# Two lows of the output projection by accumulating transfer, sums ahead of a low in the paired gates, and a pause in the early up weights

## The chip, the cores and the metric

The kernel runs on one core of a Trainium2 chip. The metric is the device time of one execution in microseconds (us), median of three runs. The engines of the core work side by side, each through an instruction queue of its own: TensorE (PE, with its weight loads as PEld), VectorE (DVE), ScalarE (ACT), GpSimd (POOL) and SyncE (SP). SP issues most transfers. POOL issues those that add to their destination.

## The reference

One layer of a hybrid backbone runs on 128 context tokens and 512 latent tokens, 640 in all, at width 1024, in f32. Cut to what matters:

```python
merged = (g_a * (y_a @ lw['w_br_a']) + g_b * (y_b @ lw['w_br_b'])
          + g_c * (y_c @ lw['w_br_c']) + g_d * (y_d @ lw['w_br_d']))
return merged @ lw['w_o'], kh, vh, s_f, s_b
...
mix, kh, vh, s_f, s_b = token_mixers(h, lw, lb_f, lb_b, ctx_k, ctx_v, s0_f, s0_b)
x = x + g1 * mix
h = rmsnorm(x, lw['norm2_g']) * (1.0 + sc2) + sh2
x = x + g2 * conv_ffn(h, lw['w_up'], lw['ffn_conv_w'], lw['ffn_conv_b'], lw['w_down'])
```

The gates `g_a` to `g_d` are sigmoids of `h @ w_gate`. The products touched by the change are the gates with their branch products, and `merged @ w_o`. After them come the second norm and the product with `w_up`.

## The kernel before

Every f32 product is made of three matmuls. An operand x is split in a high part, a copy of x in the matmul's type (ACT), and a low part, x minus the high part (DVE, `low`). High by high, high by low and low by high are summed in PSUM.

Weights come from HBM through a staging tile `raw` (three buffers, pool `rp`) into a tile `w` (three buffers, pool `wp`) that holds high and low. A raw buffer is free for the next load when both parts have been made. For some weights of the input projection the low part is made another way: `low_dma` lets ACT write minus x into the low half rounded to the matmul's type like the high half, and a transfer issued by POOL adds x to it, which leaves the remainder.

*The work list.* `units` holds a load, a preparation and a computation for each weight tile. `ahead` starts loads up to four units ahead and preparations up to two units ahead. Unless an instruction is pinned in program order, the framework's planner sets the order of each engine's queue from its own estimates; TensorE's queue also follows that planned order.

*The pair stage* (`g_all`, `g_pair`). Fourteen pairs of gate tiles are computed, each by seven block products for the gate (`gprod`, 12 matmuls) and seven small ones for the branch (`bprod`, 3 matmuls). This needs, besides the weight blocks A (the first staging tile as it is loaded) and C, sums of blocks: s0 and s1 (operand S, copied by `g_b` into B), and two further sums written over b12 and b21. While pair p runs, the operands of pair n = p + 1 are made: `g_a`, `g_sums`, `g_b`, `g_c`, `g_zh`, `g_zl`. In this stage ACT's, DVE's and POOL's instructions made through `oact`, `ovec` and `opool` are pinned in the order of the code. A pair that opens a new branch (`new`) also splits that branch's values (`y_split`), and makes g_b later.

*The output projection* (`wo_tile`). `w_o` is cut in two halves of 512 columns (nh) and four blocks of 256 rows (kk_). In the first half each block is used as it comes: its six matmuls for each of five row blocks t of 128 tokens, in five PSUM accumulators, one in a bank of the pool m, and four in two tiles of the pool g, of which row blocks 1 and 3 share one, 2 and 4 the other. With the last block the sums are read out by DVE: `wt`, the product with the gain `g1`, and the addition to x2. In the second half nothing is computed until its fourth block has come, and then each row block takes all four. Block (1,0) lies in region MG0; (1,1), (1,2) and (1,3) take the three wp buffers that (0,1), (0,2) and (0,3) leave. `R["half"]` is set when the first half's last matmul has been put in the program.

*Beside it* runs `up_early`, a generator stepped as the program is written. It prepares the first weights of the up projection ahead of time: it loads them, splits them, makes their block sums, and stores the split operands to DRAM (`upd`) in six parts, for lack of room, in regions XL0 and XL1, which are used twice. For pair 1 it waits until `half`. After each finished row block of the second half `norm2` is started: square, root, scaling into C, transposes on TensorE, modulation and split. Then `up_all` loads the next up weights by the same raw buffers.

Of the kernel before, what the change touches and what calls it, by code (L numbers as in the profile page):

```python
# [13 lines left out]
ALU = mybir.AluOpType  # L14
# [56 lines left out]
def tile_step(ctx: ExitStack, tc: tile.TileContext, a: dict, outs: list, dbg=None):  # L71
# [58 lines left out]
    def region(tag, shape, dt=F32):  # L130
        return big.tile(shape, dt, tag=tag, name=nm(tag))
# [25 lines left out]
    ovec, opool, oact = Ordered(nc.vector), Ordered(nc.gpsimd), Ordered(nc.scalar).activation  # L157
# [938 lines left out]
    def y_split():  # L1096
        bi = gx["bi"]
        c, y = gx["C"], R["y" + BR[bi]]
        src = [gx["Y"][:, i * HC:j * HC] for i, j in ((0, 2), (3, 4), (2, 3))]
        dst = [[c[:, h, 0:2].rearrange("p i t -> p (i t)"), c[:, h, 2], y[:, h, 0, HC:T]] for h in range(2)]  # L1100
        for o, x in zip(dst[0][:2], src):
            oact(o, x, AF.Copy)
        lows = [(l, x, h) for h, l, x in zip(dst[0], dst[1], src)]
        return lows[:2], lows[2]
# [26 lines left out]
    def low(w, x, h):  # L1131
        ovec.tensor_tensor(w, x, h.bitcast(F32), ALU.subtract)

    def g_a(p_, r):
        w = gw[p_, "A"] = gunit(p_, 0)
        oact(w[:, 0], r[0], AF.Copy)
        low(w[:, 1], r[0], w[:, 0])

    def g_sums(p_, r):

        s = gw[p_, "S"] = gx["S"] if p_ else region("G", [P, 2, 5, P])
        b21, (b22, b12) = r[0][:, 1], (r[1][:, 0], r[1][:, 1])
        ovec.tensor_tensor(s[:, 0], r[0][:, 0], b12, ALU.add)
        ovec.tensor_tensor(s[:, 1], s[:, 0], b22, ALU.add)
        ovec.tensor_tensor(b12, b12, b22, ALU.add)
        ovec.tensor_tensor(b21, s[:, 1], b21, ALU.add)

# [54 lines left out]
    def g_sig(p_, i, o, x):  # L1202
        bi, n = gp_id(p_)
        gc = C_BG + GI[BR[bi]] * 8 + n + 4 * i
        oact(o, x, AF.Sigmoid, bias=p1[:, gc:gc + 1])
# [24 lines left out]
    def g_pair(p_, r):  # L1230
        n, q = p_ + 1, p_ - 1
        inner, nx = p_ < GPAIR, n < GPAIR
        if not inner:
            g_sig(q, 1, gw[q, "gt", 1], gw[q, "gt", 1])
            g_close(q)
            g_merges(q)
            return
        bi, n0 = gp_id(p_)
        new = n0 == (NPL if bi == 0 else 0)
        if new:  # L1240
            gx["bi"] = bi
        if n0 == (NPL if bi == 0 else 0) + 1 and bi < 3:
            y_load(bi + 1)
        b1, b3 = pm()[:, 0:HC], pm()[:, 0:HC]
        ga = gw[p_, "gt", 0] = gp.tile([P, T], F32, tag="gt", name=nm("ga"))
        gb = gw[p_, "gt", 1] = gp.tile([P, T], F32, tag="gt", name=nm("gb"))
        g_zl(p_, r[p_])
        gprod(b1, p_, 1, True)
        if q >= 0:
            g_sig(q, 1, gw[q, "gt", 1], gw[q, "gt", 1])  # L1250
        oact(b3 if q >= 0 else ga[:, 0:HC], b1, AF.Copy)
        if q >= 0:
            g_close(q)
        ps = gw[p_, "ps"] = pg()
        p1_, p3_ = ps[:, 1, 0:HC], ps[:, 0, 0:HC]
        bprod(p1_, p_, 1, True)
        oact(p3_, p1_, AF.Copy)
        if q >= 0:
            g_merges(q)
        if nx:  # L1260
            g_a(n, r[n])
        lows, x3 = y_split() if new else ([], None)
        gprod(b3, p_, 2, q < 0)
        if q < 0:
            g_split(3, gx["t3"][0])
            ovec.tensor_tensor(ga[:, 0:HC], b3, ga[:, 0:HC], ALU.add)
        g_sig(p_, 0, ga[:, 0:HC], b3 if q >= 0 else ga[:, 0:HC])
        for x in lows:
            low(*x)
        gprod(b1, p_, 6, False)  # L1270
        oact(gb[:, 0:HC], b1, AF.Copy)
        bprod(p3_, p_, 2, False)
        b2 = pm()[:, 0:HC]
        gprod(b2, p_, 5, True)
        if nx:
            g_sums(n, r[n])
            if not new:
                g_b(n)
        gprod(b1, p_, 7, False)
        oact(gb[:, HC:T], b1, AF.Copy)  # L1280
        y = gw[p_, "y"] = gp.tile([P, T], F32, tag="gt", name=nm("y"))
        c2_ = gw[p_, "b2"] = pm()[:, 0:HC]
        bprod(p1_, p_, 6, False)
        oact(y[:, 0:HC], p1_, AF.Copy)
        bprod(c2_, p_, 5, True)
        ovec.tensor_tensor(gb[:, HC:T], b2, gb[:, HC:T], ALU.subtract)
        if new:
            g_b(n)
        if nx:
            late = g_c(n, r[n])  # L1290
            if not new:
                for x in late:
                    low(*x)
            if n + 1 < GPAIR:
                r[n + 1] = gp_load(n + 1)
        else:
            m_split(0)
            m_split(1)
        gprod(b1, p_, 4, False)
        g_sig(p_, 0, ga[:, HC:T], b1)  # L1300
        bprod(p1_, p_, 7, False)
        oact(y[:, HC:T], p1_, AF.Copy)
        if new:
            oact(x3[2], x3[1], AF.Copy)
            low(*x3)
        if nx:
            g_zh(n, r[n])
        gprod(b2, p_, 3, False)
        if n0 == (NPL if bi == 0 else 0) + 1 and bi < 3:
            y_sums()  # L1310
        ovec.tensor_tensor(y[:, HC:T], c2_, y[:, HC:T], ALU.subtract)
        ovec.tensor_tensor(gb[:, 0:HC], b2, gb[:, 0:HC], ALU.subtract)
        if new:
            for x in late:
                low(*x)

    def g_first(r):
        drain(lambda: "ada39" in R)
        g_a(0, r[0])
        g_sums(0, r[0])  # L1320
        g_b(0)
        for x in g_c(0, r[0]):
            low(*x)
        g_zh(0, r[0])
        return r
# [123 lines left out]
    for nh in range(2):  # L1449
        for kk_ in range(4):  # L1450
            plain(lambda nh=nh, kk_=kk_: rows(a["w_o"][nh, MHN[kk_]], 2, 512,
                                              "MG0" if (nh, kk_) == (1, 0) else None),
                  lambda w, nh=nh, kk_=kk_: wo_tile(nh, kk_, w))


# [46 lines left out]
    def up_early():  # L1502
        x = region("XH", [P, 5, 8, P])
        ra, r1, r2 = x[:, 0], x[:, 3], x[:, 4]
        r3 = region("XL1", [P, 8, P])
        rb = region("H", [P, 8, P])
        for r, p_, h in ((r2, 2, 0), (r3, 3, 0), (ra, 0, 0), (rb, 0, 1), (r1, 1, 0)):
            nc.sync.dma_start(r, a["w_up"][p_, h].rearrange("p a b c -> p (a b) c"))
        flat = lambda v: v.rearrange("p a b c -> p (a b) c")

        def part(hi, lo, v):
            act(hi, v, AF.Copy)
            vec.tensor_tensor(lo, v, hi.bitcast(F32), ALU.subtract)

        yield UE[0]
        for r, tag, i in ((r2, "XL0", 0), (r3, "C", 1)):
            w = region(tag, [P, 4, 4, P], F32R)
            part(flat(w[:, 0:2]), flat(w[:, 2:4]), r)
            nc.sync.dma_start(upd[i][:, 0:4], w.bitcast(F32))
            yield UE[1]  # L1520
        for p_, r, tag in ((0, ra, "MG1"), (1, r1, "S0")):
            w = up[p_, "A"] = region(tag, [P, 4, 4, P], F32R)
            part(flat(w[:, 0:2]), flat(w[:, 2:4]), r)
            yield UE[1]
        s = x[:, 1:3].rearrange("p a b c -> p (a b) c")
        q = [s[:, 4 * i:4 * i + 4] for i in range(4)]
        for p_, r, o in ((0, ra, rb), (1, r1, ra)):
            b11, b21, b22, b12 = r[:, 0:4], r[:, 4:8], o[:, 0:4], o[:, 4:8]
            while p_ and "half" not in R:
                yield 0.5  # L1530
            for y, u, v in ((q[0], b11, b12), (q[1], q[0], b22), (q[2], b12, b22)):
                z = vec.tensor_tensor(y, u, v, ALU.add)
                if p_:
                    tc.keep_in_program_order(z)
            yield UE[1 + p_]
            vec.tensor_tensor(q[3], q[1], b21, ALU.add)
            if p_ == 0:
                nc.sync.dma_start(ra, a["w_up"][1, 1].rearrange("p a b c -> p (a b) c"))
            b, c = [region(t, [P, 5, 4, P], F32R) for t in ("XL1", "XL0")]
            part(flat(b[:, 0:2]), flat(b[:, 2:4]), s[:, 0:8])  # L1540
            part(b[:, 4], c[:, 4], q[2])
            nc.sync.dma_start(upd[2 + 2 * p_], b.bitcast(F32))
            yield UE[1 + p_]
            for i, v in enumerate((q[3], b22)):
                part(c[:, i], c[:, 2 + i], v)
            nc.sync.dma_start(upd[3 + 2 * p_], c.bitcast(F32))
            yield UE[2]
        R["early"] = True
# [1002 lines left out]
```

## Time and profile before

| what | value |
|---|---|
| median of three runs | 1001.97 us (1001.49 to 1002.43) |
| the profiled execution's own time | 1002.13 us |
| its span, first to last instruction | 1000.4 us |
| granted TensorE clock | 0.998 |
| paired gates, in the span | some 309 to 526 us |
| output projection | some 525 to 584 us |

A row of a timeline gives start, length, engine, line, operation, the tile written and the tiles read, their shapes, and the number of instructions merged in it; in brackets the idle time of the engine before it and what ended that. Line 151 stands for all instructions made through the recording helper, so these are known by their tiles. Line 323 is the high part of a `w_o` tile, line 324 its low part; 1381 the matmuls of the output projection, 1391 and 1393 its read-out; 1512 and 1513 the split in `up_early`; 1180 and 1189 the matmuls of `gprod` and `bprod`; 1425 the transposes of `norm2`. A wait's row gives the total, the number of times and the longest. A transfer's row gives the number of issues, the size of each and the median time from issue to landing. The blocks of the first half appear in TensorE's rows by the region of the merged values that they multiply: E, D, B, A in turn.

### The profile page before, as it was taken

How to read it: one execution, taken by the hardware profiler on the slowest of the kernel's cores; microseconds unless marked ns; L12 is line 12 of the kernel's file. 1: busy time of each engine (PE TensorE's matmuls, PEld its weight loads, DVE VectorE, ACT ScalarE, POOL GpSimd, SP SyncE). 2: the span in 40 equal slices, each digit the busy share in tenths (PEclk: the TensorE clock that was granted, in tenths of full speed). 3: DMA queues.
4: the chain of work that ended last, by engine and by line, in shares of the span. 5: the costliest groups of instructions: out<-in, count | busy, mean ns of one | idle time of the engine just before them, and what ended most of it. 6: DMA issues, size and time to landing. Idle time of an engine off the chain costs nothing.

```text
span 1000.4 us, 18963 instructions
## 1 busy us (share of the span) xinstructions
PE 987.6 (99%) x7467; PEld 936.1 (94%) x7467; DVE 861.4 (86%) x1411; ACT 584.5 (58%) x1009; POOL 170.2 (17%) x227
## 2 busy tenths in 40 slices
PE   8999999999999999999999999999999999999997
PEld 6899999999999999999998799999999999888886
DVE  6678899878677989899879978999999998999796
ACT  6652343445555565555656476777777777756672
POOL 1000020313110223233010021222222222100004
PEclk9999999999999999999999999999999999999999
DMA  9874343498475999899448785766666666976742
GB/s 351 333 255 152 126 139 120 132 254 254 106 216 185 305 240 237 285 252 297 111 159 322 298 317 160 216 160 173 177 168 164 177 170 193 369 259 221 280 127 105
DMA packets 71016, 214.16 MB, mean 214 GB/s; under 512 B 9744, under 2 KB 24880, under 8 KB 68240
## 3 DMA queue, kind: packets, MB, share of 16 engines
q1 hardware_dynamic: 43968, 151.22, 43.1%
q0 software_dynamic: 26960, 61.75, 26.7%
q8 instruction: 58, 0.95, 0.4%
q14 instruction: 30, 0.25, 0.1%
HBM read 168.62 MB, written 48.51 MB: 217 GB/s over the span
## 4 chain that ended last, share of the span: by engine, by line
PE 91%; DVE 3%; DMA 3%; issue 1%; POOL 1%; SPq 0%; ACT 0%; POOLq 0%; ACTq 0%
PE g L1609 21%; PE m L1180 17%; PE g L375 16%; PE m L2081 9%; PE m L1609 5%; PE g L2081 4%; PE g L1189 3%; PE m L1381 3%; PE g L948 2%; PE m L1189 1%; PE m L539 1%; PE m L1604 1%; DMA B<-in_w_ada_dram 1%; DMA S<-in_w_ada_dram 1%; PE g L151 1%
## 5 line engine op out<-in xcount | busy, mean ns | idle before, releaser
L375 PE MATMUL g<-XH,w 128*128 128x320 f32 x704 | 169.4, 316 | 0.0
L375 PEld LDWEIGHTS g<-XH,w 128*128 128x128 f32 x704 | 120.3, 188 | 2.5 <-issue 1.2
L375 PE MATMUL g<-XL,w 128*128 128x320 f32 x352 | 108.7, 309 | 0.0
L1180 PE MATMUL m<-XH,w 128*128 128x320 f32 x336 | 79.8, 309 | 0.0
L375 PEld LDWEIGHTS g<-XL,w 128*128 128x128 f32 x352 | 66.3, 188 | 0.0
L2081 PE MATMUL m<-w,XH 128*128 128x512 f32 x246 | 58.5, 390 | 0.0
L1180 PEld LDWEIGHTS m<-XH,w 128*128 128x128 f32 x336 | 57.6, 188 | 0.0
L2081 PEld LDWEIGHTS m<-w,XH 128*128 128x128 f32 x246 | 46.1, 188 | 9.6
L1180 PE MATMUL m<-XL,w 128*128 128x320 f32 x168 | 51.9, 309 | 0.0
L151 ACT ACTIVATE w<-raw 128x640 fp32r<-128x640 f32 (+3 forms) x53 | 49.6, 952 | 3.2 <-PE g L375 2.0
L151 DVE TENSOR_TENSOR w<-raw,w 128x640 fp32r<-128x640 f32 (+3 forms) x43 | 44.0, 1040 | 2.6 <-ACT w L151 2.6
L151 POOL DMA_DIRECT2D wsum<-in_w_dn_dram x36 | 37.4, 1256 | 43.3 <-issue 39.4
L1180 PE MATMUL m<-X,w 128*128 128x320 f32 x264 | 42.6, 309 | 0.0
L151 DVE SCALAR_TENSOR_TENSOR X<-MG,p2t,X 128x641 f32<-128x641 f32 x44 | 38.9, 884 | 1.0 <-ACT X L151 0.2
L1180 PEld LDWEIGHTS m<-X,w 128*128 128x128 f32 x264 | 39.7, 188 | 0.0
L151 DVE SCALAR_TENSOR_TENSOR X<-X,p2t,X 128x641 f32<-128x641 f32 x44 | 38.9, 884 | 0.9
L1609 PE MATMUL g<-XL,w 128*128 128x320 f32 x240 | 38.7, 310 | 0.0
L1609 PE MATMUL g<-XL,C 128*128 128x320 f32 x240 | 38.3, 309 | 0.0
L1609 PEld LDWEIGHTS g<-XL,w 128*128 128x128 f32 x240 | 36.0, 188 | 0.6 <-ACT MG L151 0.3
L1609 PEld LDWEIGHTS g<-XL,C 128*128 128x128 f32 x240 | 36.0, 188 | 0.0
L1180 PEld LDWEIGHTS m<-XL,w 128*128 128x128 f32 x168 | 31.5, 188 | 0.0
L336 ACT ACTIVATE w<-raw 128x1024 fp32r<-128x1024 f32 (+1 forms) x22 | 24.3, 1102 | 12.3 <-PE m L948 8.2
(612 smaller groups left out, 2840.8 us busy)
## 6 DMA issues: line engine op xcount, KB each, us to landing
wsum<-in_w_dn_dram POOLq DMA_DIRECT2D x30, 512.0 KB, 11.0
raw<-in_w_up_dram SPq DMA_DIRECT2D x30, 512.0 KB, 5.2
raw<-in_w_gp_dram SPq DMA_DIRECT2D x21, 640.0 KB, 5.8
raw<-in_w_in_dram SPq DMA_DIRECT2D x19, 512.0 KB, 4.2
H<-in_w_adt_dram SPq DMA_DIRECT2D x19, 512.0 KB, 4.0
raw<-wsum SPq DMA_DIRECT2D x12, 512.0 KB, 5.5
actx<-X POOLq DMA_DIRECT2D x22, 256.0 KB, 4.8
wsum<-wsum POOLq DMA_DIRECT2D x10, 512.0 KB, 10.6
```

Source lines behind the costliest of these rows:

```text
L151: r = f(*args, **kw)
L336: high = lambda: act(w[:, 0], raw, AF.Copy)
L375: mm(o, w[:, h, k0 + k, :], r(k)[:, s], start=(k == 0 and i == 0), stop=(k == kt - 1 and i == 2))
L539: mm(m[W * g:W * g + W, (i - s0) * W:(i - s0 + 1) * W], lhs, rhs, start=True, stop=True, tile_position=(64 * par, W * g))
L948: mm(o, x(kx)[:, ts], w[:, h, k, :], start=(kx == 0 and i == 0), stop=(kx == 7 and i == 2))
L1180: mm(o, w[:, h, n, k, :], x[:, k, :], start=(first and k == 0 and j == 0), stop=(k == 3 and j == 2), skip_group_check=True)
L1189: mm(o, w[:, h, n, 4, :], x[l], start=(first and j == 0), stop=(j == 2), skip_group_check=True)
L1381: mm(m, mh[MHN[q]][:, hx, k % 2, t * P:(t + 1) * P], wo[q][:, hw, k % 2, :], start=(k == 0 and i == 0), stop=(k == 7 and i == 2))
L1604: mm(o, w[:, k, :], x[:, k, :], start=(first and not part and k == 0 and j == 0), stop=(part == 1 and k == 3), skip_group_check=True)
L1609: z = mm(o, w[:, k, :], x[:, k, :], start=(first and k == 0 and j == 0), stop=(k == 3 and j == 2), skip_group_check=True)
L2081: mm(ps, s[t // 4][:, hx, k, o:o + P], w[:, hw, k, c0:c1], start=first, stop=i == 2 and bi == len(batch) - 1 and k == len(ks) - 1, skip_gr ...
```

## The change

Three things are changed; the arithmetic of the reference stays.

- In a pair, `g_a` is cut in its ACT copy (`g_a`) and its low (`g_al`), and `g_sums` in its first two sums (`g_s01`) and its last two (`g_s23`). The first two stand where the low stood, right after the copy; in the very first pair they stand after the third operand's split. The low and the last two sums stand before product 6, after the lows of a new branch. `g_b` keeps its place.
- The blocks (1,1) and (1,2) of `w_o` get their low parts by `low_dma`.
- In `up_early`, after operand B of a pair has been split and its store issued, the generator waits for `half` before it splits and stores operand C: for pair 0 this is new, and pair 1 is past `half` already.

```diff
     def g_a(p_, r):
         w = gw[p_, "A"] = gunit(p_, 0)
         oact(w[:, 0], r[0], AF.Copy)
+
+    def g_al(p_, r):
+        w = gw[p_, "A"]
         low(w[:, 1], r[0], w[:, 0])
 
-    def g_sums(p_, r):
+    def g_s01(p_, r):
 
         s = gw[p_, "S"] = gx["S"] if p_ else region("G", [P, 2, 5, P])
+        ovec.tensor_tensor(s[:, 0], r[0][:, 0], r[1][:, 1], ALU.add)
+        ovec.tensor_tensor(s[:, 1], s[:, 0], r[1][:, 0], ALU.add)
+
+    def g_s23(p_, r):
+        s = gw[p_, "S"]
         b21, (b22, b12) = r[0][:, 1], (r[1][:, 0], r[1][:, 1])
-        ovec.tensor_tensor(s[:, 0], r[0][:, 0], b12, ALU.add)
-        ovec.tensor_tensor(s[:, 1], s[:, 0], b22, ALU.add)
         ovec.tensor_tensor(b12, b12, b22, ALU.add)
         ovec.tensor_tensor(b21, s[:, 1], b21, ALU.add)
...
         if nx:
             g_a(n, r[n])
+            if q >= 0:
+                g_s01(n, r[n])
         lows, x3 = y_split() if new else ([], None)
         gprod(b3, p_, 2, q < 0)
         if q < 0:
             g_split(3, gx["t3"][0])
             ovec.tensor_tensor(ga[:, 0:HC], b3, ga[:, 0:HC], ALU.add)
+            g_s01(n, r[n])
         g_sig(p_, 0, ga[:, 0:HC], b3 if q >= 0 else ga[:, 0:HC])
         for x in lows:
             low(*x)
+        if nx:
+            g_al(n, r[n])
+            g_s23(n, r[n])
         gprod(b1, p_, 6, False)
...
         gprod(b2, p_, 5, True)
-        if nx:
-            g_sums(n, r[n])
-            if not new:
-                g_b(n)
+        if nx and not new:
+            g_b(n)
...
             plain(lambda nh=nh, kk_=kk_: rows(a["w_o"][nh, MHN[kk_]], 2, 512,
-                                              "MG0" if (nh, kk_) == (1, 0) else None),
+                                              "MG0" if (nh, kk_) == (1, 0) else None, (nh, kk_) in ((1, 1), (1, 2))),
                   lambda w, nh=nh, kk_=kk_: wo_tile(nh, kk_, w))
...
             nc.sync.dma_start(upd[2 + 2 * p_], b.bitcast(F32))
             yield UE[1 + p_]
+            while "half" not in R:
+                yield 0.5
             for i, v in enumerate((q[3], b22)):
                 part(c[:, i], c[:, 2 + i], v)
             nc.sync.dma_start(upd[3 + 2 * p_], c.bitcast(F32))
```

More of the change, by code (lines that the diff above doesn't have):

```diff
@@ L1319, in g_first @@
         g_a(0, r[0])
-        g_sums(0, r[0])
+        g_al(0, r[0])
+        g_s01(0, r[0])
+        g_s23(0, r[0])
         g_b(0)
```

## The prediction

> **What bounds the kernel now.** I read the page's busy table first, then the windows around the stages that the change touches, then the chain of work and the timelines of the engines there. The windows have, after the stretch, its length and the busy time of PE, PEld, DVE, ACT and POOL.
>
> ```profile
> PE 987.6 (99%) x7467; PEld 936.1 (94%) x7467; DVE 861.4 (86%) x1411; ACT 584.5 (58%) x1009; POOL 170.2 (17%) x227
> ```
>
> ```profile
> 325.00:340.00 15.00, 15.00 (x104) 15.00 (x104) 14.07 (x21) 8.85 (x14) 2.99 (x5) 1.00 0.96 299
> 526.00:548.00 22.00, 22.00 (x100) 18.24 (x99) 20.48 (x23) 14.90 (x16) 0.00 (x0) 1.00 0.81 310
> 548.00:562.00 14.00, 12.81 (x57) 10.25 (x56) 13.93 (x22) 3.99 (x6) 0.00 (x0) 1.00 0.89 331
> ```
>
> TensorE sets the time: it is busy through whole stretches. So a change off TensorE is worth only the holes of PE that it closes, less those that it opens. In the stages that this change touches there is one hole, in 548 to 562, where DVE is full (13.93 of 14). PE's timeline and DVE's there:
>
> ```profile
> 547.51 2.88 PE L1381 MATMUL g<-w,A 128*128 128x512 f32 x12
> 550.24 0.84 PE L1381 MATMUL m<-w,E 128*128 128x512 f32 x3
> 552.27 3.06 PE L1381 MATMUL g<-w,A 128*128 128x512 f32 x12 [1.19 <-DVE wt L1391]
> 555.16 0.84 PE L1381 MATMUL m<-w,E 128*128 128x512 f32 x3
> 555.84 1.52 PE L1381 MATMUL m<-w,D 128*128 128x512 f32 x6
> 557.20 1.52 PE L1381 MATMUL m<-w,B 128*128 128x512 f32 x6
> ```
>
> ```profile
> 544.51 1.22 DVE L324 TENSOR_TENSOR w<-raw,w 128x1024 fp32r<-128x1024 f32 x1
> 545.65 0.69 DVE L1536 TENSOR_TENSOR XH<-XH 128x512 f32<-128x512 f32 x1
> ...
> 548.59 0.69 DVE L1513 TENSOR_TENSOR XL<-H,XL 128x512 fp32r<-128x512 f32 x1
> 549.19 0.69 DVE L1391 TENSOR_TENSOR wt<-m,F 128x512 f32<-128x512 f32 x1
> 549.79 1.22 DVE L324 TENSOR_TENSOR w<-raw,w 128x1024 fp32r<-128x1024 f32 x1
> ...
> 551.53 1.28 DVE L1391 TENSOR_TENSOR wt<-g,F 128x512 f32<-128x512 f32 x2
> ```
>
> Six 512-wide matmuls take 1.36 (555.84 to 557.20). So the three issued at 550.24 end at 550.92, and PE resumes at 552.27: 1.35 lost. The 12 after it take 2.89 (to 555.16) against 2.72: 0.17 more. The hole is worth **1.52 us**. PE waits there for row block 1 of the first half to be read out of its bank (wt at 551.53). That read is late because DVE first does weight lows (L324) and the early splits of the up weights (L1513, L1536).
>
> **The pair stage.** PE is full there (15.00 of 15). Three small holes are left, the first at 366.5. The rows are a wait of TensorE's weight loads over the whole pair stage (total, times, longest), two pieces of the chain, and the engines beside the first hole:
>
> ```profile
> PEld m L1180 <- ACT gb L151: 0.5, 3, 0.2
> ```
>
> ```profile
> 366.50 2.24 PE m L1180 x14
> 369.18 3.23 PE m L1180 x22
> ```
>
> ```profile
> 361.88 1.49 DVE L151 TENSOR_TENSOR w<-raw,w 128x1280 fp32r<-128x1280 f32 x1
> 363.29 0.82 DVE L151 TENSOR_TENSOR D<-raw,raw 128x640 f32<-128x640 f32 x1
> 365.06 1.28 ACT L151 ACTIVATE w<-D 128x1280 fp32r<-128x1280 f32 x1 [2.92 <-DVE D L151]
> ```
>
> At 22 in 3.23, fourteen matmuls take 2.06, and the piece at 366.50 took 2.24: 0.18, and three such make the 0.5 of the wait row. PE waits for the copy gb, which stands on ACT behind the copy of the sums, w<-D, which had itself waited 2.92 for DVE's sums.
>
> **The change, part by part.**
>
> *Order in a pair.* The same DVE instructions run; none is added. The two sums that g_b copies go ahead of the A low. They then end the length of that low (361.88 to 363.29, 1.41) earlier, so w<-D starts near 363.65 and gb is no longer late. Gain **0.5**. The A low comes later by the two sums, some 1.7, and is read only in the next pair, most of 15 us on: nothing. What waits behind the sums is the gb subtraction, which keeps its place: the DVE work ahead of it is the same. In the first pair the sums also pass the lows of C:
>
> ```profile
> 315.48 1.22 DVE L151 TENSOR_TENSOR C<-D,C 128x640 fp32r<-128x640 f32 x2
> 319.26 0.60 PE L1189 MATMUL g<-C,w 128*128 128x320 f32 x3
> ```
>
> Pushed by 1.7 they end at 318.4, ahead of 319.26: hidden by 0.9.
>
> *Two lows by transfer, w_o blocks (1,1) and (1,2).* Removed: the DVE rows at 544.51 and 549.79, 1.14 of pace each (544.51 to 545.65). Added: a second ACT copy for each, two transfers issued on POOL and run beside the SP's. The staging tile raw is held until its transfer has landed.
>
> ```profile
> 539.55 1.06 ACT L323 ACTIVATE w<-raw 128x1024 fp32r<-128x1024 f32 x1 [1.54 <-PE g L1381]
> ...
> 546.37 0.63 ACT L1512 ACTIVATE XL<-XH 128x512 fp32r<-128x512 f32 x1 [0.67 <-DVE XH L1536]
> 547.12 1.06 ACT L323 ACTIVATE w<-raw 128x1024 fp32r<-128x1024 f32 x1
> ```
>
> ```profile
> w<-raw POOLq DMA_DIRECT2D x6, 512.0 KB, 7.1
> w<-raw POOLq DMA_DIRECT2D x1, 512.0 KB, 4.7
> w<-raw POOLq DMA_DIRECT2D x1, 512.0 KB, 10.4
> ```
>
> *The pause in up_early.* The last two splits of up pair 0 (two of ACT at 0.63, two of DVE at 0.6 of pace), and the store behind them, go after the end of the first half. On DVE 1.2 leaves the stretch ahead of 549.19.
>
> Together: 1.14 + 1.2 leaves ahead of the first wt, which could start at 546.85. PE ends that row block at 547.51, so the reads follow PE at once. The second row block ends 1.36 later, near 548.9, and its read by 549.8, ahead of 550.92. The hole closes: **-1.52**. DVE is no longer late at that place; next late is the low of (1,2).
>
> *When that low lands.* Its tile is free when the third block's matmuls end (547.51 less the six of A at 1.36: 546.15), and ACT can begin at 546.37, as the split there has moved. Two copies of 1.06 end at 548.5. From POOL's issue such a transfer takes 4.7 to 10.4 (six of this size in the trace, median 7.1): landing at 553.2, 555.6 or 558.9. PE, without its hole, wants it at the second matmul of the B group: 557.20 - 1.52 + 0.23 = 555.9. So it is early by 2.7 at one end, late by 3.0 at the other, and early by 0.3 at the median, which I take. POOL is idle there, 0.00 in both windows above, so nothing delays the issue. Block (1,1), copied from 539.55, lands by 552.1 at worst, for 554.6. The fourth staging tile and its copies follow PE's release as before.
>
> Contention is the argument against it: the DMA share is 0.89 in that stretch. The Trainium skill, "DMA: Bandwidth & Descriptors", section "Issuing engines are not separate DMA queues", says that transfers from POOL and SP run on the same 16 engines and interleave. By it the new transfers share with the SP's stores, and the slow end, 10.4, would be the one to take, which makes the sum 3.0 worse. The landings here are split over it, as 4.7 and 10.4 stand in one run.
>
> *What comes after the half.* The moved splits, their store, and the second half of the next raw load (it waits for the low of (1,2) to land) now fall ahead of the first transposes of norm2:
>
> ```profile
> 563.79 0.69 DVE L151 TENSOR_TENSOR H<-raw,raw 128x512 f32<-128x512 f32 x1
> ...
> 567.52 0.75 DVE L1413 TENSOR_SCALAR C<-X,st 128x1024 f32<-128x1024 f32 x1 [0.47 <-POOL st L318]
> 568.76 1.03 PE L1425 MATMUL m<-cst,C 128*128 128x128 f32 x8
> ```
>
> ```profile
> upd<-XL SPq DMA_DIRECT2D x4, 1280.0 KB, 6.1
> raw<-in_w_up_dram SPq DMA_DIRECT2D x2, 512.0 KB, 9.9
> ```
>
> The transposes come 0.49 after the scaling that they read (568.27). DVE ends the stretch ahead of that 1.1 earlier than now, by the low that falls behind the half; PE comes 1.5 earlier: margin 0.1. In front of it in DVE's queue stand a split into the same region, which waits for the moved store to leave it (issued near 555.7, 6.1 to land: 561.8), and a sum that waits for raw (issued near 555.6 now, 9.9 to land as the two did: 565.5). The bounds are nothing, and 2.8: the sum at 563.79, moved 1.1 earlier, would wait from 562.7 to 565.5. SP holds its stores in order behind that load. I take **+0.8**, under a third of it: the median landings just fit, with no room, and below nothing is excluded because PE has no further hole here.
>
> Sum: -1.52 - 0.5 + 0.8 = **-1.2 us**. The profiled execution is 1002.13 us (1.73 outside its span), 0.16 above the median 1001.97, and I forecast 1000.7. About 0.2% (2.0 us) is what a measurement can tell from no change; even both holes closed with nothing lost (-2.0, 999.9) would stand on that edge.
>
> **Rivals.**
>
> *The (1,2) low lands late and PE waits (a new wait for the old).* For: slow landings of the list, traffic. Against: the median fits, the moved store frees the DMA engines, POOL is idle. At 10.4 it gives back 3.0: 999.9 + 3.0 = 1002.9, no change. PE's wait is the landing less 7.4, so the whole gain of 2.0 is gone at 9.4, and the kernel is measurably slower (1004.0) from 11.4 on, which is this rival's other side. The 512 KB transfers of the down sums show that such landings are near:
>
> ```profile
> wsum<-in_w_dn_dram POOLq DMA_DIRECT2D x30, 512.0 KB, 11.0
> ```
>
> *norm2 starts late.* The queue above blocks DVE and the transposes wait up to 2.8: up to 1002.7. For: three landings in one queue. Against: the order of each queue is planned anew.
>
> *The hole stays.* If the new order still puts DVE work in front of the reads, or PE's queue still breaks at that place, only the pair stage's 0.5 is gained: 1001.5. For: the splits of up pair 0 that remain fill DVE up to 548. Against: the 2.3 removed exceeds the 1.5 of hole.
>
> **How the numbers follow.** Forecast 0.50 (999.9 to 1001.4). Late low 0.20, of which 0.08 beyond 1004. norm2 late 0.18, of which 0.02 beyond 1004. The hole stays 0.12. The range 999.6 to 1003.0 takes the forecast with the 0.5 that the runs spread, and the rivals up to the landing of 10.4; it leaves out some 0.16. Faster by over 0.2% (under 999.97) is the forecast's lower quarter, 0.13; slower 0.10; same 0.77.
>
> **What would show it.** The wait of PE for wt gone from 550 to 552; the wait of weight loads for ACT gb gone and the pieces of 14 matmuls at 2.06; w<-raw on POOL landing before its B group; the first transposes without a wait. A wait of PE for a DMA w<-raw near 556 is the first rival; one of PE for DVE C near 567 the second. Wrong altogether would be a shift of PE's total beyond these places.

## The result: 1004.85 us, slower by 0.2%

| | before | after |
|---|---|---|
| median, on one chip | 1002.75 us (13 runs, 1001.49 to 1004.16) | 1004.85 us (13 runs, 1004.11 to 1006.66) |
| ratio | | 1.0021, 95% interval 1.0013 to 1.0029 |
| profiled execution | 1002.13 us, span 1000.4 | 1005.37 us, span 1003.5 |
| granted clock | 0.998 | 0.996 |

The sign is wrong: -1.2 us forecast, +2.1 measured, and 1004.85 lies above the range of 999.6 to 1003.0. To see where it went I count TensorE's 7467 matmul records, the same number in every trace here, and take the time between the starts of the same records. Record 3201 lies just ahead of the paired gates, 4701 near their end, 5201 in the up projection, so the third stretch holds the output projection and norm2.

| us from record to record | before | after | difference |
|---|---|---|---|
| start to 3201 | 301.81 | 301.38 | -0.43 |
| 3201 to 4701: paired gates | 220.54 | 220.00 | -0.54 |
| 4701 to 5201: output projection | 92.91 | 96.82 | +3.91 |
| 5201 to the last | 377.75 | 378.13 | +0.38 |

The first row has nothing that the change touches (it lies 300.95 to 301.63 in all thirteen other traces, so before's profiled execution was late there by chance), and the last moves by up to 1.0 between kernels that are the same in it. The pair stage gained what was forecast, 0.5. All of the loss is in the projection.

The changed kernel has other line numbers: 1393 are the matmuls of the output projection (1381 before), 1403 and 1405 its read-out, 1524 and 1525 the splits of `up_early` on ACT and DVE, 1544 and 1548 its block sums, 359 the first copy of a block whose low goes by transfer. In the runs further down they are a few lines off these. The windows of the changed kernel (length, then busy PE, PEld, DVE, ACT and POOL, granted clock, DMA share, GB/s):

```profile
526.00:548.00 22.00, 22.00 (x99) 18.21 (x98) 19.93 (x24) 14.43 (x16) 0.88 (x1) 1.00 0.85 306
548.00:562.00 14.00, 10.77 (x40) 8.06 (x39) 10.47 (x16) 4.26 (x6) 0.87 (x1) 0.88 0.96 330
```

In the stretch where 12.81 of 14 us were busy there are 10.77 now, DVE has come down from 13.93 to 10.47, and the clock from 1.00 to 0.88. DVE was relieved as intended, and TensorE waits longer. Its timeline there, and the row of its waits (m<-w,E at 551.21 and 556.04 belongs already to the second half: the program text puts it after the fourth block has come, the planner has put it between matmuls of the first half):

```profile
546.55 2.88 PE L1393 MATMUL g<-w,A 128*128 128x512 f32 x12
549.72 1.66 PE L1393 MATMUL g<-w,A 128*128 128x512 f32 x6 [0.29 <-DVE wt L1403]
551.21 0.39 PE L1393 MATMUL m<-w,E 128*128 128x512 f32 x1
554.55 1.68 PE L1393 MATMUL g<-w,A 128*128 128x512 f32 x6 [2.95 <-DVE wt L1403]
556.04 2.32 PE L1393 MATMUL m<-w,E 128*128 128x512 f32 x5
558.16 2.15 PE L1393 MATMUL m<-w,D 128*128 128x512 f32 x6
560.15 1.53 PE L1393 MATMUL m<-w,B 128*128 128x512 f32 x6
```

```profile
PE g L1393 <- DVE wt L1403: 3.2, 2, 2.9
```

The hole of 1.58 us from start to start (550.69 to 552.27) has become one of 3.34 (551.21 to 554.55): +1.76. Twelve matmuls from 546.55 would end at 549.27 and the next start at 549.72: +0.45. And after the hole, eight matmuls follow each other at 0.427 us instead of 0.227 (five at 556.04 take until 558.16): +1.6. These three make 3.8 of the 3.9. DVE's queue says why:

```profile
544.10 0.68 DVE L1525 TENSOR_TENSOR XL<-H,XL 128x512 fp32r<-128x512 f32 x1
544.70 0.68 DVE L1548 TENSOR_TENSOR XH<-XH 128x512 f32<-128x512 f32 x1
545.30 2.43 DVE L1525 TENSOR_TENSOR XL<-XH,XL 128x1024 fp32r<-128x1024 f32 x3
547.65 0.68 DVE L1403 TENSOR_TENSOR wt<-m,F 128x512 f32<-128x512 f32 x1
...
548.98 0.68 DVE L1403 TENSOR_TENSOR wt<-g,F 128x512 f32<-128x512 f32 x1
552.60 0.69 DVE L1544 TENSOR_TENSOR XH<-XH 128x512 f32<-128x512 f32 x1 [2.93 <-DMA XH<-in_w_up_dram]
553.21 0.68 DVE L1405 TENSOR_TENSOR X<-X,wt 128x512 f32<-128x512 f32 x1
553.81 0.68 DVE L1403 TENSOR_TENSOR wt<-g,F 128x512 f32<-128x512 f32 x1
```

Two things are to be seen. The splits that were to wait for the half (L1525) stand ahead of the first read-out all the same: the planner moved them up again. And between the second read-out and the third stands the first sum of up pair 1 (L1544), which waits 2.93 us for a load. In before's queue no such row stood among the read-outs. The third read-out, for which TensorE waits, is stuck behind it. The transfers behind this (from issue to landing), and ACT's two copies of block (1,2), the high part and minus x:

```profile
XH<-in_w_up_dram SPq DMA_DIRECT2D x1, 512.0 KB, 7.1
w<-raw POOLq DMA_DIRECT2D x1, 512.0 KB, 10.2
```

```profile
547.58 1.06 ACT L359 ACTIVATE w<-raw 128x1024 fp32r<-128x1024 f32 x1 [1.53 <-DMA raw<-in_w_o_dram]
548.55 1.04 ACT L151 ACTIVATE w<-raw 128x1024 fp32r<-128x1024 f32 x1
```

The load for the sum was issued at 545.45 and takes 7.1: 552.5, where the sum starts. The low of (1,2) was issued at 549.89, 1.4 later than forecast, because ACT had to wait for the raw block, and took 10.2: it landed at 560.1, just where the B group began (560.15). So a second late thing lay hidden behind the first.

### The profile page after: what moved, and what is told of

The parts are those of the page before. It is cut to its first block, busy times and chain, and to the rows that moved or that the text cites. A ratio compares the mean times of both kernels' runs of the same rounds, so it can differ in the third digit from the quotient of the medians.

```text
span 1003.5 us, 18971 instructions
## 1 busy us (share of the span) xinstructions
PE 989.1 (99%) x7467; PEld 936.8 (93%) x7467; DVE 858.8 (86%) x1409; ACT 587.4 (59%) x1011; POOL 171.4 (17%) x229
## 4 chain that ended last, share of the span: by engine, by line
PE 88%; DVE 6%; DMA 3%; issue 2%; POOL 1%; ACT 0%; SPq 0%; POOLq 0%; DVEq 0%; ACTq 0%
PE g L1623 19%; PE m L1186 17%; PE g L375 15%; PE m L2095 9%; PE g L2095 4%; PE g L1195 3%; PE m L1393 3%; PE m L1623 3%; PE g L948 2%; PE m L151 2%; PE g L151 1%; PE m L1195 1%; DVE X L151 1%; PE m L539 1%; PE m L1618 1%
## 5 line engine op out<-in xcount | busy, mean ns | idle before, releaser
L151 ACT ACTIVATE w<-raw 128x640 fp32r<-128x640 f32 (+3 forms) x55 | 51.9, 956 | 3.4 <-PE g L375 2.0
L151 ACT ACTIVATE gb<-m 128x320 f32<-128x320 f32 x28 | 12.3, 438 | 43.1 <-PE m L1186 43.1
## 6 DMA issues: line engine op xcount, KB each, us to landing
wsum<-wsum POOLq DMA_DIRECT2D x10, 512.0 KB, 10.5
```

Source lines behind the costliest of these rows:

```text
L151: r = f(*args, **kw)
```

## The experiments

The theory after reading the trace: the low of (1,2) is late in itself (L), and the sum between the read-outs (Q) only covers it. The rival: Q alone. Each run was compared with runs of the kernel before on the same chip (medians 1002.25 for the runs whose names begin with e, 1002.51 for f and g, 1002.82 for h). The ratio is not the quotient of the two medians (in e_pairs_pause that would be 1.0004). The column of the projection is the stretch from record 4701 to 5201, 92.91 in before and 96.82 after the change; like every row shown, it comes from the one execution that was profiled.

| run | median us | ratio, 95% interval | projection us |
|---|---|---|---|
| e_pairs | 1001.71 | 0.9995, 0.9985 to 1.0004 | 94.02 |
| e_pairs_pause | 1002.70 | 0.9997, 0.9987 to 1.0007 | 93.20 |
| e_pairs_low11 | 1002.16 | 0.9998, 0.9989 to 1.0006 | 93.62 |
| e_pairs_lows | 1007.84 | 1.0049, 1.0037 to 1.0061 | 99.13 |
| f_early | 1009.19 | 1.0063, 1.0051 to 1.0075 | 101.93 |
| g_meant | 1006.96 | 1.0044, 1.0031 to 1.0057 | 98.88 |
| g_lows01 | 1007.11 | 1.0047, 1.0035 to 1.0059 | 98.05 |
| g_act | 1000.07 | 0.9977, 0.9967 to 0.9988 | 92.11 |
| h_meant11 | 1002.02 | 0.9995, 0.9987 to 1.0004 | 93.50 |
| h_quiet | 1002.99 | 1.0004, 0.9991 to 1.0017 | 93.24 |
| h_actonly | 1000.58 | 0.9976, 0.9967 to 0.9984 | 91.44 |
| h_best | 999.88 | 0.9972, 0.9961 to 0.9983 | 91.96 |

### The parts one by one

**e_pairs**: the new order in the pairs alone; the lows of (1,1) and (1,2) stay on DVE, and there is no pause.

```diff
-  rows(a["w_o"][nh, MHN[kk_]], 2, 512, ..., (nh, kk_) in ((1, 1), (1, 2)))
+  rows(a["w_o"][nh, MHN[kk_]], 2, 512, ...)
-            while "half" not in R:
-                yield 0.5          # before the splits of operand C
```

> Only the new order in a pair; both lows stay on DVE, no pause. Queue theory (the loss is one sum of up pair 1 that DVE's queue now holds between the read-outs, waiting for its reload) and landing theory (the (1,2) low by transfer lands too late, but stood behind that hole): both expect the pair stage's three waits gone and the 1.5 us hole near 551 as before, about -0.5 us against the kernel before. A rival, that the pair order itself costs time later, expects +1 or more.

The median is 0.5 below before's, as expected, but the interval includes no change. The pair stage is 220.00 as in the full change. The profiled execution, 1003.11 and so 1.4 above the median, has a projection 1.1 longer than before's: TensorE comes 1.1 earlier to the hole at 550, and the hole ends when it did (2.72 from 549.55 to 552.26). What fixes that end can be read from TensorE, ACT and DVE:

```profile
552.26 3.04 PE L1393 MATMUL g<-w,A 128*128 128x512 f32 x12 [2.33 <-DVE wt L1403]
```

```profile
529.55 1.06 ACT L1524 ACTIVATE C<-XL 128x1024 fp32r<-128x1024 f32 x1 [2.92 <-DMA XL<-in_w_up_dram]
530.83 1.06 ACT L1524 ACTIVATE XL<-XH 128x1024 fp32r<-128x1024 f32 x1 [0.22 <-DMA XH<-in_w_up_dram]
531.79 1.26 ACT L151 ACTIVATE B<-MG 128x1280 fp32r<-128x1280 f32 x1
```

```profile
533.09 1.49 DVE L151 TENSOR_TENSOR B<-MG,B 128x1280 fp32r<-128x1280 f32 x1 [2.66 <-ACT B L151]
```

ACT waits for a load of up weights with the copy of the merged values (B<-MG) behind it, DVE waits for that copy, and then is full up to the read-outs. The row B<-MG of DVE stood at 533.08 in before too, where the hole ended at 552.27; in e_pairs_pause, the next run, it stands at 532.41 and the hole ends at 551.59. In all three the hole ends 19.2 after this row, so a TensorE that comes earlier only waits longer. The row itself follows the load: that was issued 1.1 earlier in e_pairs than in before (521.54 against 522.68), but took 8.0 us to land against 6.8.

**e_pairs_pause** (the order and the pause) and **e_pairs_low11** (the order and the low of (1,1) by transfer):

> Pair order and pause, both lows on DVE. The first sum of up pair 1 stands in DVE's queue after the fourth read-out, which comes after its reload has landed. Queue theory: no new wait, as the pair order alone, -0.5 us (within 0.4). If the pause itself costs, +1 or more; no transfer of a low is in it, so the landing theory expects -0.5 as well.

> Pair order, no pause, only block (1,1)'s low by transfer; (1,2)'s low on DVE, where it now stands ahead of the first read-out. The transfer of (1,1) has some 3 us to spare even if it takes 11. Both theories: no wait for a transfer; the DVE hole near 551 stays in part, 0.3 to 1.2 us, for DVE does the (1,2) low first. -0.8 to -1.7 us against before.

Neither changes the time measurably, so the 0.5 of the one and the 0.8 to 1.7 of the other are not to be seen. With the pause the hole is 1.88, and the first sum of pair 1 starts at 553.89 without a wait, so the pause alone does no harm. With (1,1) the hole is 1.47, over the 0.3 to 1.2 expected, the transfer lands in 9.4 us with nobody waiting, and 0.45 is lost at the first transposes of norm2.

**e_pairs_lows**: the order and both lows by transfer, no pause.

```diff
-            while "half" not in R:
-                yield 0.5          # before the splits of operand C
```

> The changed kernel without the pause in up_early. In DVE's queue the five read-outs now follow each other and the sums of up pair 1 come after them. Queue theory alone: the DVE hole is gone and nothing takes its place, -2.0 us against before. Landing theory: TensorE now waits at the B group of the first row block of the second half for the transfer into w, which lands some 10 us after issue near 549, 3 to 4 us late: +1 to +2 us against before.

```profile
555.47 0.39 PE L1393 MATMUL m<-w,B 128*128 128x512 f32 x1
560.27 2.50 PE L1393 MATMUL m<-w,B 128*128 128x512 f32 x5 [4.41 <-DMA w<-raw]
```

Without the pause no sum stands among the read-outs, the five of them follow each other, and the hole at 550 is gone (0.54 from start to start). The time is worse than with the whole change. TensorE now waits 4.41 us for the low of (1,2), at the second matmul of the B group, which is the first to use it; and 11 of the matmuls after it run at 0.427 us. The expectation had the place, and was short by 3 us or more on the price.

### Are two waits stacked?

**f_early**: the whole change, with the load for pair 1's sums moved so early that the sum finds its data.

```diff
             nc.sync.dma_start(upd[i][:, 0:4], w.bitcast(F32))
+            if i == 0:
+                nc.sync.dma_start(r2, a["w_up"][1, 1]...)
-        for p_, r, o in ((0, ra, rb), (1, r1, ra)):
+        for p_, r, o in ((0, ra, rb), (1, r1, r2)):
-            if p_ == 0:
-                nc.sync.dma_start(ra, a["w_up"][1, 1]...)
```

> The changed kernel with one thing different: the second half of up pair 1 is loaded into the place of the first staging tile, right after that tile has been split, instead of into ra after the sums of pair 0. So the first sum of pair 1, which stood between the read-outs and waited 2.93 us for this load, finds its data there. Theory A (that wait is all that was wrong): the DVE hole of PE goes, and the kernel comes to some 1000, 2 under before. Theory B (two late things were stacked, and the wait for the sum hid the landing of the low of block (1,2)): PE now waits for the transfer w<-raw at the B group of the second half, 3.5 to 5 us near 556, as with the pair order and both lows but no pause (4.4 there), and the time is again 1005 to 1008.

```profile
550.98 1.06 ACT L359 ACTIVATE w<-raw 128x1024 fp32r<-128x1024 f32 x1 [5.35 <-DMA raw<-in_w_o_dram]
```

```profile
556.22 0.39 PE L1393 MATMUL m<-w,B 128*128 128x512 f32 x1
562.28 2.50 PE L1393 MATMUL m<-w,B 128*128 128x512 f32 x5 [5.68 <-DMA w<-raw]
```

The wait of the sum is gone and the kernel is slower still, beyond even the 1005 to 1008 of theory B. It is no clean test: the low of (1,2) lands later than in the changed kernel (562.3 against 560.1), since the raw load of that block, with the early load beside it, took 11.9 us to land (8.1 in the changed kernel), and a hole of 1.97 is left at 549, as sums of pair 1 now stand ahead of and between the read-outs. That Q alone doesn't explain the loss rests on e_pairs_lows, where no sum is in the way, and on the next run.

**g_meant**: DVE's order as the prediction described it.

```diff
-            vec.tensor_tensor(tmp, m, grows["g1"][:, v, cs], ALU.mult)
+            z = vec.tensor_tensor(tmp, m, grows["g1"][:, v, cs], ALU.mult)
+            if nh == 0:
+                tc.keep_in_program_order(z)
...          # and the DVE splits of operand C pinned likewise
```

> The changed kernel with DVE's order as the prediction described it: the five read-outs of the first half are pinned, and the last splits of operand C of up pair 0 and the sums of pair 1 are pinned behind them. If the order of DVE was the only step that failed, this is the predicted kernel: no hole at 550, 1000.7. If the landing of the low of (1,2) failed too (issue 549.8 and 10 us to land in the changed kernel, against the 548.5 and 7.1 of the prediction), PE waits 4 to 5 us for w<-raw near 556, some 12 matmuls after it run at 0.427 instead of 0.227 us, and the time is 1006 to 1008.

```profile
554.48 0.39 PE L1393 MATMUL m<-w,B 128*128 128x512 f32 x1
558.48 2.50 PE L1393 MATMUL m<-w,B 128*128 128x512 f32 x5 [3.62 <-DMA w<-raw]
560.78 2.76 PE L1393 MATMUL m<-w,A 128*128 128x512 f32 x6
563.34 2.17 PE L1393 MATMUL m<-w,E 128*128 128x512 f32 x6
```

This is the kernel that the prediction priced, and it takes 1007, not 1000.7. There is no hole at 550, so closing it was priced rightly; the low by transfer is what fails. It was issued at 548.98, 0.5 later than forecast, and landed 9.5 us later. The stall is 4.00 from start to start, a matmul's 0.23 and 3.8 lost, and the six matmuls at 563.34 still take 2.17, against 1.52 at full pace.

### Why the low is late

**h_quiet**: g_meant, with the store of operand B of up pair 0 (1280 KB) moved from beside that transfer to behind the read-outs, with the last split of B ahead of it (its copy is then made by DVE).

```diff
-            part(b[:, 4], c[:, 4], q[2])
-            nc.sync.dma_start(upd[2 + 2 * p_], b.bitcast(F32))
...          # for pair 0 both are written after the splits of C
```

> Both lows by transfer and DVE's order as the prediction described it; in addition the store of operand B of up pair 0 (1280 KB, issued at 546.7, 8.8 us to land) is made to come after the read-outs, behind the next raw loads, so that it doesn't run beside the transfer of the low of (1,2). If that transfer is slow because it shares the DMA engines, it lands in 5 to 7 us from its issue near 549.0, PE waits under 1.5 us near 555 in place of 3.6, and no slow pace follows: 1001.5 to 1004. If some 9.5 us is what it takes whatever runs beside it, PE's wait stays at 3.5 to 4 us: 1006 to 1008.

The transfer's row in g_meant, then in h_quiet, for issues after 548; and TensorE of h_quiet:

```profile
w<-raw POOLq DMA_DIRECT2D x1, 512.0 KB, 9.5
```

```profile
w<-raw POOLq DMA_DIRECT2D x1, 512.0 KB, 5.1
```

```profile
554.58 1.52 PE L1393 MATMUL m<-w,B 128*128 128x512 f32 x6
...
567.60 1.09 PE L1439 MATMUL m<-cst,C 128*128 128x128 f32 x8 [1.30 <-DVE C L1427]
```

Issued at 549.11, it lands in 5.1 us instead of 9.5, and TensorE doesn't wait for it at all; of the 4.4 us that g_meant's median lies over before's, 0.2 are left. So the transfer was slow because of what ran beside it: between 549.1 and 554.2 the DMA engines moved 382 GB/s in g_meant and 207 in h_quiet. The Trainium skill, "DMA: Bandwidth & Descriptors", section "Issuing engines are not separate DMA queues", says that transfers started by different engines run on the same 16 engines and interleave; these two rows agree with that. What is left is the other rival: the first transposes wait 1.30 us for norm2's scaling, because what was put behind the half stands ahead of it on DVE. The twelve runs of h_quiet reach from 1001.66 to 1007.74, wider than any other kernel's here. The two upper ones, 1007.46 and 1007.74, have g_meant's time and its granted clock (0.995, against 0.997 to 0.999 in the other ten). A low that lands late again in them would look like this, but no trace of them shows it.

**h_meant11**: g_meant with the low of (1,2) on DVE, so only (1,1) by transfer.

> The change with DVE's order as the prediction described it (read-outs pinned, last splits of pair 0 behind them), but the low of block (1,2) stays on DVE; only (1,1) goes by transfer. If the late low of (1,2) was the one step that failed, this one loses its 3.6 us wait of PE and the slow pace behind it: DVE has 2.3 us less ahead of the read-outs less the 1.1 of the low that is back, so no hole over 0.6 us at 550, and 1000.0 to 1001.5. If the landing of (1,1) or what was moved behind the half (the sums that wait for the second half of the next up weights, 6 us on DVE with both lows) takes the gain, over 1002.

```profile
547.62 1.23 DVE L324 TENSOR_TENSOR w<-raw,w 128x1024 fp32r<-128x1024 f32 x1 [1.92 <-ACT w L323]
```

```profile
550.83 3.01 PE L1393 MATMUL g<-w,A 128*128 128x512 f32 x12 [1.36 <-DVE wt L1403]
```

The 3.6 us wait is gone as expected, but the time is 1002.02, over the 1000.0 to 1001.5: a hole of 1.75 stays at 550 (1.58 in before), and 0.44 is lost at norm2 besides. The low of (1,2), back on DVE, stands ahead of the first read-out and itself waits 1.92 us, through ACT's copy, for the raw block. That load was issued at 538.48, before the work that was taken off DVE, so it comes no sooner.

**g_lows01**: pair order, and the lows of (1,0) and (1,1) by transfer, those with time to spare.

```diff
-  (nh, kk_) in ((1, 1), (1, 2))
+  (nh, kk_) in ((1, 0), (1, 1))
```

> Pair order as changed, no pause, and the two lows by transfer are those of the blocks (1,0) and (1,1) instead of (1,1) and (1,2). Their copies on ACT start near 534 and 538.5, so at 10.5 us a landing they are there by 547 and 551, ahead of the second half at 552. DVE loses 2.28 us of lows ahead of the first read-out. If what a low by transfer costs is only when it lands, PE waits for none, the hole at 550 shrinks from 2.7 to under 0.6 us, and the kernel comes to 999.5 to 1000.5, 2 under before. If traffic or what comes behind (norm2, the next raw loads) takes it back, 1001.5 to 1003, as with (1,1) alone (1002.2).

```profile
raw<-in_w_o_dram SPq DMA_DIRECT2D x1, 512.0 KB, 11.5
```

```profile
551.40 1.23 DVE L324 TENSOR_TENSOR w<-raw,w 128x1024 fp32r<-128x1024 f32 x1 [5.52 <-ACT w L323]
552.55 0.68 DVE L1403 TENSOR_TENSOR wt<-m,F 128x512 f32<-128x512 f32 x1
```

```profile
553.88 2.82 PE L1393 MATMUL g<-w,A 128*128 128x512 f32 x6 [4.78 <-DVE wt L1403]
```

I expected 999.5 to 1000.5, or 1001.5 to 1003 by the rival, and got 1007.11. No TensorE wait for a low is left, but the two transfers (issued 537.2 and 540.6, 9.6 to land) run beside the raw load of (1,2), issued at 538.71, and that lands after 11.5 us, against 7.2 in before. ACT's copy waits for it, DVE's low for ACT, and all read-outs for that low: 5.17 from start to start. The lateness has moved from the low to a load. That the transfers slowed it is inferred from what ran beside it; no run takes only one of them away.

### What sets the hole at 550

**g_act**: pair order; ACT copies the merged values ahead of the up weights. **h_actonly**: the same on the kernel before, without the pair order.

```diff
+        fixed[0] = True      # pins ACT's copies
         m_split(2)
         m_split(3)
+        fixed[0] = False
...  # in up_early: loads in the order ra, r1, r2, r3, rb; first four copies pinned
```

> Pair order as changed, nothing by transfer and no pause; ACT's order after the gates is changed: the copies of the merged values (B<-MG, A<-MG) go ahead of the copies of the up weights, whose loads land at 529.5 and 530.8 and held ACT for 2.92 us (the loads are given in the order ra, r1, r2, r3, rb, and these copies are pinned). Theory: the hole of PE at 550 ends when DVE's queue has been worked off, and that queue starts from B<-MG; then DVE's row B<-MG moves from 533.1 to 530.3, all behind it by 2 to 2.7, the hole shrinks from 2.7 to under 0.7, and the kernel comes to 999.3 to 1000.3. Rival: the queue is held again further on (the store of XL that has to land by 541.8, the loads of w_o), and the hole keeps over 1.5: 1001 to 1002.

> The kernel before with only ACT's order changed (merged values ahead of the up weights), without the new order in the pairs. If the gain of the pair stage (1.1 us earlier at the projection) was given back at the hole of DVE in the run of the pair order alone, then ACT's order alone closes the hole of 1.5 and gives 1000.6 to 1001.0, and the pair order adds its 0.9 to it (1000.1 with both). If the pair order is worth nothing, this one is as fast as both together, 999.9 to 1000.2.

ACT, DVE and TensorE of g_act, and the window of h_actonly:

```profile
527.76 1.28 ACT L151 ACTIVATE B<-MG 128x1280 fp32r<-128x1280 f32 x1 [1.21 <-DVE MG L151]
```

```profile
530.25 1.48 DVE L151 TENSOR_TENSOR B<-MG,B 128x1280 fp32r<-128x1280 f32 x1
```

```profile
550.29 3.01 PE L1395 MATMUL g<-w,A 128*128 128x512 f32 x12 [0.45 <-DVE wt L1405]
```

```profile
548.00:562.00 14.00, 14.00 (x63) 11.45 (x63) 13.93 (x21) 3.80 (x5) 0.00 (x0) 1.00 0.83 313
```

DVE starts on B<-MG at 530.25 instead of 533.09, with no instruction and no transfer saved, and its wait of 2.66 is gone. The raw block (1,2) comes earlier too: DVE frees its staging tile sooner, and the load is issued at 534.3 instead of 539.8 and lands at 538.0 instead of 547.0. In h_actonly the hole closes entirely: TensorE is busy 14.00 of 14, and the projection takes 91.44, 1.47 less than before. In g_act TensorE arrives 0.5 earlier and loses 0.61 at the hole (0.84 from start to start), which fits the two equal ratios: the 0.5 of the pair order is real (220.00 against 220.51) and is given back there.

**h_best**: pair order, ACT's order, the read-outs pinned ahead of the last splits of up pair 0, no low by transfer.

> Pair order, ACT's order, the read-outs pinned ahead of the last splits of up pair 0, and no low by transfer: two parts of the change with the failed one left out. With ACT's order alone a hole of 0.6 us was left at 550, where two splits and a low of w_o stood ahead of the second read-out. They are behind it here, so no hole: 999.2 to 999.7. If what is moved behind the half delays norm2, as with the pinned order and both lows (0.86 lost at 572.6), 1000 to 1001.

```profile
549.71 2.98 PE L1395 MATMUL g<-w,A 128*128 128x512 f32 x12
...
567.47 1.09 PE L1441 MATMUL m<-cst,C 128*128 128x128 f32 x8 [0.27 <-DVE C L1429]
```

999.88, 0.28% under before and the fastest here, though its interval overlaps those of g_act and h_actonly. The hole at 550 is closed, and 0.43 comes back at norm2 (0.66 from start to start), a little over the 999.2 to 999.7 expected, by the reason given for 1000 to 1001. It has no low by transfer; those were never tried with ACT's new order.

## Why the prediction was wrong, point by point

**Right.** The pair stage: 0.5 forecast, 0.54 measured, and the waits for gb are gone. The hole: worth 1.52 by forecast, 1.47 by h_actonly (which closes it by another change). POOL was idle, and the transfer was issued 0.3 us after its copy had ended (548.55 and 1.04, then 549.89). The rival "the (1,2) low lands late and PE waits" named the right transfer and the right matmul, and "norm2 starts late" the right instruction: 0.63 in g_meant, 1.46 in h_quiet (1.69 from start to start) and 0.43 in h_best, against the 0.8 taken.

**Wrong: the pause moves the splits.** The planner put them ahead of the read-outs all the same (544.10 and 545.30). What the pause did was to change what else it could place there.

**Wrong: "DVE is no longer late at that place".** I counted the work taken out ahead of the read-outs, and took the order among them as it was. The planner put a sum there whose load needs 7.1 us from 545.45, and DVE waited 2.93 us for it. In the changed kernel the hole is 3.34 with this sum among the read-outs; in e_pairs_lows, with the same two lows taken out and no sum there, it is 0.54.

**Wrong: when the low of (1,2) lands.** This is the term that would have decided even without the sum (g_meant). Taken: issue 548.5, landing 7.1 later, 0.3 early. Measured in g_meant: issue 548.98, landing 9.5 later, a wait of 3.62. Of the 3.8 lost, 0.5 is the later issue, 2.4 the longer landing, and 1.2 that TensorE wanted the low sooner, at 554.7 and not 555.9, less the 0.3 of margin. Of this 1.2, some 0.5 is the pair order's own gain, which the sum counted but left out of this time; the rest is that g_meant came 0.7 earlier to the gates than before's profiled execution. The issue was wrong because ACT's copy waits for the raw block. In the profile of before, that load was issued at 539.83; its row among the transfers:

```profile
raw<-in_w_o_dram SPq DMA_DIRECT2D x1, 512.0 KB, 7.2
```

So it landed at 547.0, and ACT could not begin at 546.37. No wait showed it there, since ACT was busy until then. The duration was wrong because I took the median of transfers elsewhere in the program, which run beside other traffic. The argument that I set aside, the shared engines, was the deciding one (5.1 against 9.5).

**Wrong: the price of a long wait.** A late landing was priced at its lateness. Here are the stalls of TensorE in this stage, from start to start, with the intervals of over 0.3 us between the matmuls that follow (the first interval after a stall is always among them, with 0.32 to 0.59):

| stall us | 1.47 to 1.97 (six traces) | 2.72 | 3.34 | 4.00 | 4.79 | 5.17 | 6.07 |
|---|---|---|---|---|---|---|---|
| intervals over 0.3 us after it | 1 or 2 | 1 | 9 | 14 | 13 | 8 | 13 |
| cost of these, us | 0.1 to 0.3 | 0.1 | 1.7 | 3.0 | 2.6 | 1.7 | 2.8 |

So a stall of 3.3 us or more costs 1.7 to 3.0 on top of itself here. The bound that I gave, "measurably slower from 11.4 on" for the landing, left that out, with the earlier want: in g_meant the low landed 9.5 after its issue, and the kernel was slower by 0.44%.

**A chance.** Faster than 999.97 was given 0.13 as the lower quarter of the forecast, but of its 1.5 us (999.9 to 1001.4) only 0.07 lie there: the chance was too high for the range it was taken from.

## What to carry to other kernels

An engine's load in a window doesn't say what is late in it: ask of each instruction that stands ahead of the awaited one what it waits for itself, loads too, and expect a planner to fill a gap with an instruction that waits. Work handed from a busy engine to transfers is paid in transfers: a load beside two of them took 11.5 us in place of 7.2 (g_lows01), and in windows whose mean DMA share was 0.83 to 0.96, such a 512 KB transfer took 5.1 to 10.5 us. The share alone doesn't tell which: the fast one stood at 0.92 (h_quiet), the one of 9.5 us at 0.83 (g_meant). If a hole moves neither with the work ahead of it nor with the time of arrival, follow the late engine's queue back to the first row at which it waited; here it was a copy on ACT behind a load, and a new order of ACT's copies and of the loads gained 2.2 us, where the three parts of the change cost 2.1.

## What I had not expected of the hardware

The slow pace after a stall begins between 2.7 and 3.3 us in these traces: after stalls of up to 2.72 the matmuls run at 0.227 us, and from 3.34 on 7 to 13 of them at 0.427, at a granted clock of 0.88 in the window of the changed kernel. The Trainium skill, "TensorE: Matmul & The Clock Gate", section "Part 1: The HAM clock gate", gives half the rate after an idle window of about 3.4 us, and 426.7 ns for a cold matmul of 512 columns. The trace agrees with the cold pace. With the threshold it agrees nearly: the shortest of the stalls with a slow pace behind it, 3.34 us, had 2.95 us of idle time in the profile, a little less than that window. That the number of slow matmuls does not grow with the stall agrees with the free-running window of the same section, but no run here tries that.
